# Hybrid backbone, one core: the instruction order planned by the scheduler's timeline model

## The chip, the cores and the metric

The kernel runs on one core of one Trainium2 chip. Such a core has a matrix engine (TensorE, PE in the profile), three engines for element-wise work (VectorE = DVE, ScalarE = ACT, GpSimd = POOL), a queue engine that here only issues transfers (SyncE = SP), and 16 DMA engines. Each engine works through its own instruction list strictly in the order in which the program gives it; engines wait for each other by semaphores. The metric is the device time of the launch in microseconds (us); the kernel before takes 1644.6 us, the median of 3 runs (1644.48 to 1645.88).

## What is computed

Two layers of a transformer-like trunk, over 256 context tokens and 1024 latent tokens of width 1024, in float32. Layer 0 mixes tokens by windowed attention with grouped heads, layer 1 by multi-head latent attention (MLA). Cut to what matters here:

```python
def reference(x, c, ctx, c_ctx, ...):
    for i in range(DEPTH):                       # DEPTH = 2
        shift_x, scale_x, gate_x = adaln(c, ada_w[i], ada_b[i])
        hx = rms_norm(x, norm_g[i]) * (1.0 + scale_x[:, None]) + shift_x[:, None]
        hc = rms_norm(ctx, norm_g[i]) * (1.0 + scale_c) + shift_c
        if kind == 0:
            yx, yc = window_gqa(hx, hc, ...)     # layer 0
        elif kind == 1:
            yx, yc = latent_attention(hx, hc, ...)   # layer 1
        x = x + gate_x[:, None] * yx
    return rms_norm(x, final_g)

def latent_attention(...):                       # 16 heads, keys = ctx and latent tokens
    def attend(qn, qr, kn, kr, v):
        s = (jnp.einsum("bqhd,bkhd->bhqk", qn, kn)
             + jnp.einsum("bqhd,bkd->bhqk", qr, kr)).astype(F32) * scale
        p = jax.nn.softmax(s, axis=-1).astype(v.dtype)
        return jnp.einsum("bhqk,bkhd->bqhd", p, v)
```

## The kernel before

The kernel is written for Tile, a layer that records the instructions of a Python function, finds from the memory that each reads and writes what it depends on, and plans when the block closes: it lets a modelled clock run and gives each engine, whenever the model has it free, the ready instruction that stands first in the source. The result is a fixed list per engine, with semaphore waits between them. The model of time is thus what decides where the lists depart from the order of the source.

On-chip memory is cut by hand: one float32r area (`arena_r`), one float32 area (`arena_f`), small columns (`small`) and all eight banks of the accumulator memory as one tensor (`PB`). Products that need full precision are made of two float32r halves (`split`: a cast on ACT at L120, the rest by a subtraction on DVE or POOL at L121) and three matmuls (`mm3`, L125, L126, L127). The stages in order, with the stretch of the profiled span that each takes:

- 0 to 66 us, the start: the conditioning product (`ada_mm`, L301) waits for `ada_w` pieces from memory; tokens are loaded (L175), normalised, turned (L187).
- 66 to 366 us: layer 0's projections (`proj_a`, `proj_t`), weights loaded at L227; beside them DVE sums up the rest of the conditioning (L362, with its loads at L341).
- 366 to 729 us: windowed attention, 40 units (tile of 128 queries, group of 4 heads). Per unit: scores (L569, L570), their maximum on DVE (L576), exponential on ACT (L579), turning of the probabilities on PE (`T`, L597), cast and rest (L120, L121), the product with V (`PV`, L607). The output product of the tile before (`outproj`, three matmuls at a time through L125 to L127) is dealt out between them as filler, in eight portions of six matmuls per tile.
- 729 to 1013 us: layer 1's projections.
- 1013 to 1561 us: MLA, 32 units (head, half of the queries). Per unit ten chunks of 128 keys: scores of 128 keys by 512 queries (L1188, through `mm3`), exponential on ACT (L1190), sum on POOL (L1194, L1197). Ahead of that, for the unit after next or the next one, the `top` products (L1171) and their maximum (L1175 on DVE), turned at L1179. At the end the product with V (L1205), whose two accumulators sit in the upper and lower 64 rows of one bank.
- 1561 to 1646 us: the last output product and the final norm.

In MLA the product with V is 10 plain float32 matmuls, one per chunk, with 64 columns of weights each; even chunks use the columns 0 to 63 of the array, odd ones the columns 64 to 127. In the source they stand together, behind the tenth score:

```python
        def PV(self):
            self.pv = psv()
            for c in range(NT):
                p = 64 * (c % 2)
                nc.tensor.matmul(
                    self.pv[p : p + 64], Vq[:, c, self.h % 4, :], self.E.pop(c), start=c < 2, stop=c >= NT - 2
                )
...
            u.score(c)
...
            if c == 9:
                u.PV()
                u.fin()
```

`Er` holds ten exponentials, the scores turn through three banks (`pst4`), the product with V has one bank (`psv`, bank 6), and `fin` (L1219 on ACT, L1220 on DVE) empties it.

## Time and profile before

| what | value |
|---|---|
| median of 3 runs | 1644.6 us (1644.48 to 1645.88) |
| profiled execution, its own time | 1647.77 us |
| its span, first to last instruction | 1645.9 us |
| granted TensorE clock, mean | 0.990 |
| DVE / ACT / POOL busy | 964.1 / 825.2 / 792.5 us |
| bytes moved | 176.75 MB, mean 107 GB/s |

The profiled execution is 3.2 us longer than the median, and its span is 1.9 us shorter than its own time. PE has most of the span; the other three are busy for about half of it. A matmul in the records is longer than the distance to the next one, since they are pipelined, so the price of a matmul is read from one start to the next. A plain float32 matmul (L1205, L301) leaves two records in the trace, every other one leaves one.

### The profile page before, as it was taken

What the parts mean: (1) busy time and instruction counts of PE and PEld (TensorE: products, weight loads), DVE (VectorE), ACT (ScalarE), POOL (GpSimd) and SP (SyncE); (2) the same over time, 40 slices, a digit from 0 to 9 for tenths busy, and PEclk for the clock granted to TensorE, in tenths of its full rate; (3) what the DMA queues carried; (4) which work ended last, traced back from release to release, by engine and by line L of the source; (5) the groups of instructions that cost most, each with busy time, mean ns of one, the idle gap of its engine ahead of it and who ended that gap; (6) DMA issues with size and microseconds to landing.
All of it is one profiled execution on the core that took longest, in us unless ns stands there. A gap on an engine that the chain in (4) does not pass through costs nothing.

```text
span 1645.9 us, 23722 instructions
## 1 busy us (share of the span) xinstructions
PE 1587.9 (96%) x8156; PEld 1215.5 (74%) x8156; DVE 964.1 (59%) x1972; ACT 825.2 (50%) x1779; POOL 792.5 (48%) x776
## 2 busy tenths in 40 slices
PE   6899999999999999998999999999999999999998
PEld 2687778887878888878887887566756756666687
DVE  1797853539888888869454015655555455455354
ACT  3622112249777777777333334555555555555421
POOL 1444426224453333345254423686676777668510
PEclk9899999999999999999999999999999999999999
DMA  8557665364343333334127713111111111122151
GB/s 280 165 154 204 180 206 141 94 178 124 93 119 94 91 90 90 90 113 160 52 90 251 222 61 103 61 55 33 39 40 34 45 40 35 49 77 69 47 160 65
DMA packets 127202, 176.75 MB, mean 107 GB/s; under 512 B 11100, under 2 KB 69084, under 8 KB 127080
## 3 DMA queue, kind: packets, MB, share of 16 engines
q1 hardware_dynamic: 124920, 171.12, 34.4%
q10 hardware_dynamic: 2160, 4.11, 0.8%
q8 instruction: 64, 1.05, 0.3%
q14 instruction: 58, 0.48, 0.1%
HBM read 129.04 MB, written 46.15 MB: 106 GB/s over the span
## 4 chain that ended last, share of the span: by engine, by line
PE 70%; DVE 11%; ACT 6%; issue 6%; POOL 3%; DMA 3%; SPq 0%; ACTq 0%; DVEq 0%; POOLq 0%
PE PB L125 15%; PE PB L127 15%; PE PB L126 15%; PE PB L1205 9%; PE PB L1171 4%; PE PB L607 3%; PE PB L597 3%; DVE arena_f L362 2%; DVE arena_r L121 2%; PE PB L569 2%; DVE arena_f L576 1%; PE PB L570 1%; ACT arena_f L579 1%; DMA arena_f<-ada_w 1%; ACT arena_r L120 1%
## 5 line engine op out<-in xcount | busy, mean ns | idle before, releaser
L125 PE MATMUL PB<-arena_r 128*128 128x512 f32 (+3 forms) x1632 | 608.1, 373 | 5.7 <-ACT arena_r L204 3.8
L126 PE MATMUL PB<-arena_r 128*128 128x512 f32 (+3 forms) x1632 | 599.2, 368 | 4.0 <-DVE arena_r L206 3.6
L127 PE MATMUL PB<-arena_r 128*128 128x512 f32 (+3 forms) x1632 | 597.0, 368 | 0.2 <-DVE arena_r L121 0.2
L125 PEld LDWEIGHTS PB<-arena_r 128*128 128x128 f32 (+1 forms) x1632 | 311.2, 191 | 95.3 <-issue 30.3
L1197 POOL TENSOR_TENSOR arena_f<-arena_f 128x512 f32<-128x512 f32 x252 | 326.9, 1297 | 76.4 <-ACT arena_f L1190 61.3
L127 PEld LDWEIGHTS PB<-arena_r 128*128 128x128 f32 (+1 forms) x1632 | 310.9, 191 | 50.3 <-issue 0.9
L126 PEld LDWEIGHTS PB<-arena_r 128*128 128x128 f32 (+1 forms) x1632 | 312.2, 191 | 45.9 <-DVE arena_r L206 4.7
L1190 ACT ACTIVATE arena_f<-PB 128x512 f32<-128x512 f32 x320 | 188.9, 597 | 126.6 <-PE PB L127 114.7
L1175 DVE TENSOR_REDUCE arena_f<-PB 128x1 f32<-128x1280 f32 x128 | 190.5, 1488 | 105.4 <-PE PB L1171 102.9
L121 DVE TENSOR_TENSOR arena_r<-PB,arena_r 128x512 fp32r<-128x512 f32 (+4 forms) x255 | 162.3, 644 | 114.8 <-ACT arena_r L120 113.1
L121 POOL TENSOR_TENSOR arena_r<-arena_f,arena_r 128x512 fp32r<-128x512 f32 x84 | 117.6, 1412 | 153.5 <-ACT arena_r L120 106.5
L120 ACT CAST arena_r<-PB 128x512 fp32r<-128x512 f32 (+4 forms) x255 | 137.7, 549 | 66.6 <-PE PB L597 27.8
L576 DVE CUSTOM_DVE_ANT_0 arena_f<-PB,arena_f,small 128x256 f32<-128x256 f32 (+1 forms) x288 | 145.8, 523 | 28.1 <-PE PB L570 21.9
L1205 PE MATMUL PB<-arena_f 128*64 128x512 f32 x640 | 157.1, 600 | 0.0
L579 ACT ACTIVATE arena_f<-arena_f,small 128x640 f32<-128x640 f32 (+2 forms) x160 | 119.3, 747 | 28.8 <-DVE small L578 27.9
L120 ACT CAST arena_r<-arena_f 128x512 fp32r<-128x512 f32 (+2 forms) x132 | 78.3, 609 | 105.5 <-DMA arena_f<-a_w_in 21.3
L607 PE MATMUL PB<-arena_r 128*128 128x512 f32 x336 | 123.3, 441 | 4.3 <-ACT arena_f L618 3.2
L597 PE MATMUL PB<-ident,arena_f 128*128 128x128 f32 x672 | 110.6, 274 | 1.0 <-ACT arena_f L579 0.8
L1205 PEld LDWEIGHTS PB<-arena_f 128*64 128x64 f32 x640 | 43.5, 136 | 80.9 <-issue 79.7
L1171 PE MATMUL PB<-arena_r 96*128 96x512 f32 (+1 forms) x384 | 99.8, 368 | 2.0 <-DVE arena_f L1175 1.9
L362 DVE SCALAR_TENSOR_TENSOR arena_f<-arena_f,small 128x512 f32<-128x512 f32 x98 | 87.7, 942 | 17.7 <-DMA arena_f<-ada_w 17.5
L597 PEld LDWEIGHTS PB<-ident,arena_f 128*128 128x128 f32 x672 | 83.3, 140 | 19.3 <-ACT arena_f L579 4.7
(149 smaller groups left out, 1768.7 us busy)
## 6 DMA issues: line engine op xcount, KB each, us to landing
arena_r<-q_d SPq DMA_DIRECT2D x80, 256.0 KB
arena_f<-ada_w SPq DMA_DIRECT2D x68, 256.0 KB
arena_f<-a_w_in SPq DMA_DIRECT2D x40, 256.0 KB
q_d<-arena_f SPq DMA_DIRECT2D x80, 128.0 KB
arena_f<-x SPq DMA_DIRECT2D x16, 512.0 KB
qn_d<-arena_f SPq DMA_DIRECT2D x16, 512.0 KB
arena_r<-qn_d SPq DMA_DIRECT2D x32, 256.0 KB
arena_f<-ada_w SPq DMA_DIRECT2D x14, 512.0 KB
```

What stands on the lines that cost most here:

```text
L120: nc.scalar.copy(hi, src)
L121: (lo_eng or nc.vector).tensor_sub(lo, src, hi.bitcast(F32))
L125: nc.tensor.matmul(o, ah, bh, start=first, stop=False)
L126: nc.tensor.matmul(o, al, bh, start=False, stop=False)
L127: nc.tensor.matmul(o, ah, bl, start=False, stop=last)
L597: nc.tensor.transpose(pt[:, h, :], self.Ps[h][:, ci * 128 : ci * 128 + 128], ident)
L607: nc.tensor.matmul(self.pv, V[:, self.chunks[ci], self.g, :], PT[:, s], start=ci == 0 and s == 0, stop=ci == self.m - 1 and s == 1,)
L1171: nc.tensor.matmul(psm[:, n0 : n0 + n], self.qT[0:96, 0, b * 128 : b * 128 + 128], kt[0:96, 0, n0 : n0 + n], start=True, stop=True,)
L1175: nc.vector.reduce_max(self.mx[:, 96 + b : 97 + b], psm[:, 0:TOK], AX.X, negate=True)
L1190: nc.scalar.activation(E, S, AF.Exp)
L1197: eng.tensor_add(self.acc, self.acc, E)
L1205: nc.tensor.matmul(self.pv[p : p + 64], Vq[:, c, self.h % 4, :], self.E.pop(c), start=c < 2, stop=c >= NT - 2)
```

## The change

One argument of the context is set. Nothing in the kernel's function changes: the same 12744 instructions that do work or transfers, on the same engines, with the same operands.

```diff
-    with tile.TileContext(nc) as tc:
+    with tile.TileContext(nc, schedule_with_timeline_sim=True) as tc:
         tile_hybrid_backbone_kernel(tc, t, out)
```

With it the planner's clock is that of a model with a timeline for all engines, in place of the simpler one. Where an engine's next instruction by the source isn't ready by that clock, a later one is drawn ahead. Of PE's 7790 matmuls 5282 change their place, by 14 places on average over all; in the windowed attention by 30. Of 772 instructions on POOL 217 move, of 658 transfers on SP 313, most by a place or two.

PE in MLA, one unit (L125 to L127 are the three matmuls of one score, L1171 a `top`, L1205 the product with V). Before:

```order
L127 MATMUL PB<-arena_r 128x512
L1171 MATMUL PB<-arena_r 128x512 x2
L1171 MATMUL PB<-arena_r 128x256
L1205 MATMUL PB<-arena_f 64x512 x10
L125 MATMUL PB<-arena_r 128x512
L126 MATMUL PB<-arena_r 128x512
L127 MATMUL PB<-arena_r 128x512
L1171 MATMUL PB<-arena_r 128x512 x2
L1171 MATMUL PB<-arena_r 128x256
```

The ten products with V stand in one piece. Changed, the same engine and stage:

```order
L127 MATMUL PB<-arena_r 128x512
L1205 MATMUL PB<-arena_f 64x512
L125 MATMUL PB<-arena_r 128x512
L126 MATMUL PB<-arena_r 128x512
L127 MATMUL PB<-arena_r 128x512
L1205 MATMUL PB<-arena_f 64x512
L125 MATMUL PB<-arena_r 128x512
L126 MATMUL PB<-arena_r 128x512
L127 MATMUL PB<-arena_r 128x512
L1205 MATMUL PB<-arena_f 64x512
L1171 MATMUL PB<-arena_r 128x512 x2
L1171 MATMUL PB<-arena_r 128x256
```

Products with V are drawn between the scores as soon as their exponential is there, mostly one at a time. Over all 320 of them: before, 55 pieces (23 of ten, 2 of nine, 7 of six, 7 of two, 16 of one); now 218 pieces (3 of four, 22 of three, 49 of two, 144 of one), with even and odd chunks still taking turns.

PE in the middle of the windowed attention (L125 to L127 are the output product of the tile before, L569 and L570 a score, L597 turns, L607 the product with V, L626 turns the reciprocals). Before:

```order
L607 MATMUL PB<-arena_r 128x512 x2
L125 MATMUL PB<-arena_r 128x512
L126 MATMUL PB<-arena_r 128x512
L127 MATMUL PB<-arena_r 128x512
L125 MATMUL PB<-arena_r 128x512
L126 MATMUL PB<-arena_r 128x512
L127 MATMUL PB<-arena_r 128x512
L569 MATMUL PB<-arena_r 128x256
L570 MATMUL PB<-arena_r 128x256
L569 MATMUL PB<-arena_r 128x384
L570 MATMUL PB<-arena_r 128x384
L597 MATMUL PB<-ident,arena_f 128x128 x4
```

Now:

```order
L607 MATMUL PB<-arena_r 128x512
L125 MATMUL PB<-arena_r 128x512
L569 MATMUL PB<-arena_r 128x256
L570 MATMUL PB<-arena_r 128x256
L626 MATMUL PB<-ident,arena_f 128x128 x2
L126 MATMUL PB<-arena_r 128x512
L127 MATMUL PB<-arena_r 128x512
L125 MATMUL PB<-arena_r 128x512
L126 MATMUL PB<-arena_r 128x512
L127 MATMUL PB<-arena_r 128x512
L607 MATMUL PB<-arena_r 128x512
L597 MATMUL PB<-ident,arena_f 128x128 x2
```

The filler no longer comes in sixes at set places: it stands 73 places earlier on average, its longest piece is 19 matmuls instead of 6, and the two halves of a product with V can be parted.

SP at the start (L294 loads `ada_w`, L175 a tile of tokens, L227 layer 0's weights):

```order
 L227 DMA arena_f<-a_w_in 128x2x256 x2
+L294 DMA arena_f<-ada_w 128x2x512 x3
 L175 DMA arena_f<-x 128x1024
-L294 DMA arena_f<-ada_w 128x2x512 x4
+L294 DMA arena_f<-ada_w 128x2x512
 L175 DMA arena_f<-x 128x1024
-L294 DMA arena_f<-ada_w 128x2x512 x2
-L227 DMA arena_f<-a_w_in 128x2x256 x2
-L294 DMA arena_f<-ada_w 128x2x512 x2
+L294 DMA arena_f<-ada_w 128x2x512
+L227 DMA arena_f<-a_w_in 128x2x256 x2
```

Three of the `ada_w` pieces are issued ahead of a tile of tokens.

## The prediction

> **What bounds the kernel now.** First the page: engines, then the chain that ended last.
>
> ```profile
> span 1645.9 us, 23722 instructions
> PE 1587.9 (96%) x8156; PEld 1215.5 (74%) x8156; DVE 964.1 (59%) x1972; ACT 825.2 (50%) x1779; POOL 792.5 (48%) x776
> PE 70%; DVE 11%; ACT 6%; issue 6%; POOL 3%; DMA 3%; SPq 0%; ACTq 0%; DVEq 0%; POOLq 0%
> ```
>
> PE is busy for 96% of the span and holds most of the chain. A new order adds or removes no work, so it can act in two ways only: on PE's idle time, and on what the same matmuls cost beside other neighbours. The table of windows gives the first by stage (stretch, its length, then busy time of PE, PEld, DVE, ACT, POOL, granted clock, DMA share, GB/s):
>
> ```profile
> 0.00:66.00 66.00, 47.69 (x215) 24.86 (x216) 24.09 (x47) 27.23 (x52) 17.08 (x26) 0.90 0.71 241
> 66.00:366.00 300.00, 289.28 (x1537) 241.95 (x1536) 187.09 (x292) 80.80 (x147) 117.97 (x89) 0.98 0.58 164
> 366.00:729.00 363.00, 353.25 (x2080) 298.00 (x2080) 307.08 (x1060) 289.48 (x720) 153.51 (x214) 1.00 0.34 96
> 729.00:1013.00 284.00, 276.00 (x1422) 233.82 (x1421) 120.35 (x231) 114.56 (x235) 109.03 (x127) 0.99 0.43 139
> 1013.00:1561.00 548.00, 543.83 (x2542) 351.66 (x2541) 283.06 (x282) 293.22 (x583) 386.81 (x300) 1.00 0.16 51
> 1561.00:1646.00 85.00, 77.82 (x370) 65.24 (x368) 42.47 (x65) 19.90 (x44) 8.13 (x22) 0.99 0.34 111
> ```
>
> PE idles 18.3 us at the start, 10.7 in layer 0's projections, 9.8 in the windowed attention, 8.0 in layer 1's projections, 4.2 in MLA and 7.2 at the end. That is all that a better order can win: 46.8 us ahead of MLA, and next to nothing in MLA, where PE has work for 543.8 of 548 us. MLA is the longest stage, and there any matmul that gets dearer goes straight onto the end, since ACT with 293 and POOL with 387 busy microseconds have room.
>
> **What a product with V costs, alone and in company.** The changed order breaks the 320 products with V (L1205) from 55 pieces into 218. The timeline of PE shows pieces of one, two, six and ten in the kernel before (start, length, line; two records per matmul on L1205), the chain of waits a piece of nine:
>
> ```profile
> 1058.61 0.39 PE L127 MATMUL PB<-arena_r 100*128 100x512 f32 x1
> 1058.93 1.07 PE L1205 MATMUL PB<-arena_f 128*64 128x512 f32 x2
> 1059.93 0.31 PE L1179 MATMUL PB<-ident,arena_f 128*100 128x128 f32 x1
> ...
> 1062.20 2.80 PE L1205 MATMUL PB<-arena_f 128*64 128x512 f32 x12
> 1064.92 0.50 PE L125 MATMUL PB<-arena_r 100*128 100x512 f32 x1
> 1065.26 0.39 PE L126 MATMUL PB<-arena_r 100*128 100x512 f32 x1
> 1065.49 0.40 PE L127 MATMUL PB<-arena_r 100*128 100x512 f32 x1
> 1065.82 1.07 PE L1205 MATMUL PB<-arena_f 128*64 128x512 f32 x2
> 1066.82 0.50 PE L125 MATMUL PB<-arena_r 100*128 100x512 f32 x1
> 1067.15 0.39 PE L126 MATMUL PB<-arena_r 100*128 100x512 f32 x1
> 1067.38 0.40 PE L127 MATMUL PB<-arena_r 100*128 100x512 f32 x1
> 1067.71 1.08 PE L1205 MATMUL PB<-arena_f 128*64 128x512 f32 x4
> 1068.72 0.72 PE L1171 MATMUL PB<-arena_r 96*128 96x512 f32 x2
> ...
> 1078.82 4.51 PE L1205 MATMUL PB<-arena_f 128*64 128x512 f32 x20
> 1083.26 0.50 PE L125 MATMUL PB<-arena_r 100*128 100x512 f32 x1
> ```
> ```profile
> 1043.83 4.43 PE PB L1205 x18
> ```
>
> Read from the start of a piece to the start of what follows: one product takes 1.00 us (1058.93 to 1059.93, and again 1065.82 to 1066.82), two take 1.01, six 2.72, ten 4.44, and nine 4.43. One costs what two cost, and nine what ten cost. So an even and an odd chunk that stand next to each other run at the same time, in the two halves of the array, for 0.86 us the pair ((4.44 - 2.72) / 2 pairs); a product without a neighbour of the other half holds the array for the same 0.86. Each piece ends with another 0.15 (2.72 - 3 x 0.86 = 0.14, 4.44 - 5 x 0.86 = 0.14, 1.00 - 0.86 = 0.14). At its front the matmul ahead gets longer too: L127 to L1205 takes 0.32 and 0.33 us (1058.61 to 1058.93, 1065.49 to 1065.82, 1067.38 to 1067.71), L126 to L127 0.23, so 0.10 more. A piece of n products thus costs 0.25 us + 0.86 us x (n/2, rounded up).
>
> The Trainium skill has a rule that speaks against such an order: by "TensorEngine Tiling (Array Packing)", section "Key Properties", different tiles of the array compute in parallel, but a change of the tiling mode drains TensorE. The 0.25 us per piece agree with a drain; without one, the sum below would be 63.6 us instead of 104.4.
>
> **The sum for MLA.** Before: 23 pieces of ten, 2 of nine, 7 of six, 7 of two, 16 of one are 115 + 10 + 21 + 7 + 16 = 169 array times and 55 pieces: 169 x 0.86 + 55 x 0.25 = 159.1 us. As a check: a piece's own length in the timeline is 0.07 longer than the distance to the next start (1.07 for 1.00, 4.51 for 4.44), so without the 0.10 ahead of it L1205 should be busy 169 x 0.86 + 55 x 0.22 = 157.4 us. Its row in the table of windows has 157.1; the two rows under it are used below:
>
> ```profile
> 1013.00:1561.00 548.00, 157.06 (x640) 43.55 (x640) 1.00 0.16 51
> L1175 DVE TENSOR_REDUCE arena_f<-PB 128x1 f32<-128x1280 f32 x128 | 190.5, 1488 | 105.4 <-PE PB L1171 102.9
> L1190 ACT ACTIVATE arena_f<-PB 128x512 f32<-128x512 f32 x320 | 188.9, 597 | 126.6 <-PE PB L127 114.7
> ```
>
> Now: 144 of one, 49 of two, 22 of three, 3 of four are 144 + 49 + 44 + 6 = 243 array times and 218 pieces: 243 x 0.86 + 218 x 0.25 = 263.5 us. The difference is 74 x 0.86 + 163 x 0.25 = 63.6 + 40.8 = **+104.4 us** of PE time. Pieces of three do not occur in the trace; if their third product cost only half a pair, 22 x 0.43 = 9.5 us go off, so the term lies between 95 and 104. I take 103, since nine cost what ten do, and no cover exists: ACT waits 126.6 us for PE at L1190 and DVE 105.4 at L1175 (rows above), so neither is what PE would have waited for. Of PE's 4.2 idle microseconds here some 3 should go, since a score now stands further behind the exponential that empties its bank: **-3**.
>
> **The rest of the program.** The filler of the windowed attention is bunched. What PE waits for there are short chains, a cast and a subtraction behind each turn:
>
> ```profile
> L121 DVE TENSOR_TENSOR arena_r<-PB,arena_r 128x512 fp32r<-128x512 f32 (+4 forms) x255 | 162.3, 644 | 114.8 <-ACT arena_r L120 113.1
> L120 ACT CAST arena_r<-PB 128x512 fp32r<-128x512 f32 (+4 forms) x255 | 137.7, 549 | 66.6 <-PE PB L597 27.8
> L301 PE MATMUL PB<-arena_f,small 128*2 128x512 f32 x64 | 23.1, 663 | 7.8 <-DMA arena_f<-ada_w 7.8
> ```
>
> In the new order a few products with V stand right behind the turn that they need (the piece shown in the part on the change has L607 after a single one of two L597 groups); each such place costs up to the 0.55 us of a cast. On the other side the order draws scores ahead of the turns. DVE is the second engine of that stage, 307 of 363 us, so a stretch without filler shows as waiting. From below, all of the 9.8 idle microseconds go; from above, one cast per unit, 40 x 0.55 = 22 us. Nearer to the lower end in kind, since most places keep a whole chain between: I take **+3**. At the start PE waits 7.8 us for `ada_w`; three pieces of it now go ahead of a tile of tokens, which is then late instead: the bytes that the first 66 us need stay the same, and they move at 241 GB/s there. From -8 (that wait gone) to +8 (moved to the turns): **0**. The projections' stages keep their order nearly everywhere (counted in the two orders, 299 of the 1518 matmuls of layer 0's move): 0, from -9 to +9, half of their 18.7 idle microseconds.
>
> **Sum.** 103 - 3 + 3 = +103 us. On the profiled execution's own 1647.8 us that makes 1750.6; it is 3.2 us above the median, so **1747 us** beside 1644.6, 6% slower.
>
> **The rivals.**
>
> *The idle time is won back.* The timeline model follows all engines, and its order may fit the chip better ahead of MLA, with less waiting. There are 46.8 us to win; the start's 18.3 hang on transfers and hardly move, so half of the total is much: -23. 1747 - 23 - 3 (the windowed attention's) = 1721 us. Against it: the idle time there is spread over short waits that the kernel's own interleaving of the source already aimed at.
>
> *The windowed attention starves.* The filler is gone where the chains are long; at a cast per unit, 22 us instead of 3, and as much as half of 18.7 in the projections: 1747 + 19 + 9 = 1775 us.
>
> *The array pairs them anyway: not slower.* If an odd product could still overlap its even partner across the three matmuls of a score between them, the 63.6 us of lost pairing and most of the 40.8 would vanish, and with 23 us of idle time won the time would be 1644.6 - 23 + (0 to 20) = 1622 to 1642 us. It decides from about 80% of the term on. The rows at 1065.82 and 1067.71 speak against it: there an odd product stands three matmuls ahead of the next ones, just as in the new order, and each piece pays in full. By the Trainium skill, "TensorE: Matmul & The Clock Gate", section "The mechanism", weight loads may be pulled ahead but matmuls start and end in strict order; those rows agree.
>
> That the change does nothing is excluded by the order itself.
>
> **How the numbers follow.** Forecast (1735 to 1760): 0.76. Idle time won back: 0.10. Starved attention: 0.11. Paired anyway: 0.03. The range of 8 in 10 takes in the term's lower bound (95 instead of 103) together with most of the won idle time, and most of the starved case: 1720 to 1770 us. Anything beyond 0.2% (3.3 us), about what a measurement of this kernel can tell from no change, counts: faster 0.02, same 0.01, slower 0.97.
>
> **What would show it.** In the profile after: L1205's busy time in MLA near 257 us instead of 157 (243 x 0.86 + 218 x 0.22); single L1205 rows with 1.00 us to the next start; MLA some 100 us longer with PE busy almost throughout; the stages ahead of it within 10 us of their lengths. Wrong would be: pieces of one that take 0.43, an MLA stage of 548 us, or more than 20 us moved ahead of it.

## The result, and the profile after

| | median us | ratio to before, 95% interval |
|---|---|---|
| before | 1644.54 (4 runs) | |
| timeline model | 1797.17 (1796.0 to 1797.94, 4 runs) | 1.0928 [1.0909, 1.0947] |

The change costs 152.6 us. The forecast was slower, but by 103 us, and its range ended at 1770. The page of the profiled execution (1796.5 us) begins so:

```profile
span 1794.7 us, 23680 instructions
PE 1709.8 (95%) x8156; PEld 1214.4 (68%) x8156; DVE 950.7 (53%) x1972; ACT 830.9 (46%) x1779; POOL 790.1 (44%) x776
```

The other engines work as long as before (DVE 951 for 964 us, ACT 831 for 825, POOL 790 for 793). PE's busy time grows by 122 us with the same 8156 records, and its idle time from 58 to 85. The row of the products with V on the same page, and their busy time in MLA from the table of windows (stretch, length, PE, PEld, clock, DMA share, GB/s):

```profile
L1205 PE MATMUL PB<-arena_f 128*64 128x512 f32 x640 | 255.5, 615 | 0.0
```
```profile
1016.70:1703.90 687.20, 254.89 (x638) 49.30 (x640) 1.00 0.12 37
```

255.5 us instead of 157.1: the forecast was 257. The granted clock in MLA is 1.00 here as in the kernel before, so it is not the clock that makes them dearer. What one piece costs stands in the timeline of PE (start, length, line, count; two records per product):

```profile
1242.98 0.40 PE L127 MATMUL PB<-arena_r 100*128 100x512 f32 x1
1243.30 1.07 PE L1205 MATMUL PB<-arena_f 128*64 128x512 f32 x2
1244.31 0.50 PE L125 MATMUL PB<-arena_r 100*128 100x512 f32 x1
1244.64 0.39 PE L126 MATMUL PB<-arena_r 100*128 100x512 f32 x1
1244.87 0.40 PE L127 MATMUL PB<-arena_r 100*128 100x512 f32 x1
1245.20 1.07 PE L1205 MATMUL PB<-arena_f 128*64 128x512 f32 x2
...
1259.41 1.93 PE L1205 MATMUL PB<-arena_f 128*64 128x512 f32 x6
1261.27 0.50 PE L125 MATMUL PB<-arena_r 100*128 100x512 f32 x1
```

One product again takes 1.00 us to the next start (1243.30 to 1244.31 in rounded rows; all 144 pieces of one lie between 1.002 and 1.004), three take 1.86 (1259.41 to 1261.27). The matmul ahead takes 0.32 instead of 0.23 (1242.98 to 1243.30), as forecast. So does, and this the forecast left out, the one behind: L125 to L126 is 0.33 (1244.31 to 1244.64), L126 to L127 0.23. A piece between scores thus costs 0.35 us beside its array times, not 0.25.

The second surprise stands at the end of a unit. This is the timeline of PE, ACT and DVE around the turn L1179, first in the kernel before (rows of other lines left out):

```profile
1214.26 0.27 PE L1179 MATMUL PB<-ident,arena_f 128*100 128x128 f32 x1
1214.29 0.47 PE L127 MATMUL PB<-arena_r 100*128 100x512 f32 x1
1214.60 0.76 PE L1171 MATMUL PB<-arena_r 96*128 96x512 f32 x3
1214.69 1.12 ACT L1182 ACTIVATE arena_r<-PB,ident 4x128 fp32r<-4x128 f32 x4
1215.29 4.51 PE L1205 MATMUL PB<-arena_f 128*64 128x512 f32 x20
...
1219.73 0.50 PE L125 MATMUL PB<-arena_r 100*128 100x512 f32 x1
```

and then in the changed one:

```profile
1186.78 0.27 PE L1179 MATMUL PB<-ident,arena_f 128*100 128x128 f32 x1
1186.81 0.84 PE L1171 MATMUL PB<-arena_r 96*128 96x512 f32 x3
1187.58 1.12 ACT L1182 ACTIVATE arena_r<-PB,ident 4x128 fp32r<-4x128 f32 x4
1187.68 1.49 DVE L1175 TENSOR_REDUCE arena_f<-PB 128x1 f32<-128x1280 f32 x1 [1.03 <-PE PB L1171]
1188.75 0.50 PE L125 MATMUL PB<-arena_r 100*128 100x512 f32 x1 [1.11 <-ACT arena_r L1182]
```

L1179 turns the maxima of the next unit's scores; ACT writes them in four steps into that unit's queries (L1182), and only then can its first score start. Before, the ten products with V stood between turn and score, 4.4 us of work. Now they have been drawn ahead, one `top` of 0.6 us is left, and PE stands for 1.11 us. The waits of PE (waiter, awaited line, total us, times, longest) show it 20 times:

```profile
PE PB L125 <- ACT arena_r L1182: 21.1, 20, 1.9
```

In the kernel before, PE has no wait at L1182 among its groups. The table of windows shows the same, and more (stretch, length, PE, PEld, DVE, ACT, POOL, clock, DMA share, GB/s):

```profile
722.00:950.00 228.00, 212.42 (x1082) 180.78 (x1082) 99.99 (x207) 98.01 (x201) 96.54 (x115) 0.97 0.45 147
950.00:1036.00 86.00, 79.52 (x363) 59.65 (x361) 29.57 (x34) 31.42 (x57) 24.27 (x21) 0.94 0.28 87
1036.00:1679.00 643.00, 619.82 (x2377) 321.19 (x2376) 259.07 (x256) 273.64 (x541) 363.27 (x285) 1.00 0.12 35
```

In MLA (the last row) PE idles 23.2 us, where the kernel before had 4.2. In the stages ahead of it PE idles 15.6 and 6.5 us, and the granted clock is 0.97 and 0.94; in the kernel before the stretches 719 to 949 and 949 to 1020 us have 8.7 us at 0.99 and 0.2 us at 1.00.

By stage, with each matmul's time up to the next matmul's start given to the stage that its source line belongs to (us; the trace's rows laid beside the program's order, the same rule for all kernels below; the head of MLA is what the source puts between layer 1's projections and the loop over the 32 units):

| stage | before | after | difference |
|---|---|---|---|
| start | 61.5 | 57.4 | -4.1 |
| layer 0's projections | 299.8 | 291.6 | -8.2 |
| windowed attention | 363.2 | 363.6 | +0.4 |
| layer 1's projections | 223.5 | 232.8 | +9.3 |
| head of MLA | 61.6 | 69.4 | +7.8 |
| MLA | 535.7 | 675.5 | +139.8 |
| end | 88.6 | 92.9 | +4.3 |

MLA has 140 of 149 us. By the prices read off: 74 array times x 0.86 = 63.6; 163 pieces x 0.25 = 40.8 (as forecast), x 0.10 behind them = 16.3; the wait at L1182 21.1. That is 141.8, 2 us more than measured.

### The profile page after: what moved, and what is told of

It is laid out like the page before. It is cut to its first block, busy times and chain, and to the rows that moved or that the text cites. A ratio compares the mean times of both kernels' runs of the same rounds, so it can differ in the third digit from the quotient of the medians.

```text
span 1794.7 us, 23680 instructions
## 1 busy us (share of the span) xinstructions
PE 1709.8 (95%) x8156; PEld 1214.4 (68%) x8156; DVE 950.7 (53%) x1972; ACT 830.9 (46%) x1779; POOL 790.1 (44%) x776
## 4 chain that ended last, share of the span: by engine, by line
PE 52%; ACT 2%; DVE 2%; DMA 1%; issue 1%; POOL 0%; SPq 0%; POOLq 0%; ACTq 0%; DVEq 0%
PE PB L1205 13%; PE PB L125 12%; PE PB L126 11%; PE PB L127 11%; PE PB L1171 4%; ACT arena_r L1182 1%; PE PB L1230 1%; DVE arena_f L201 1%; PE PB L1248 0%; DVE arena_r L206 0%; DMA arena_f<-b_w_out 0%; ACT arena_r L120 0%; DMA arena_f<-b_w_in 0%; DVE arena_f L1175 0%; ACT arena_f L1219 0%
## 5 line engine op out<-in xcount | busy, mean ns | idle before, releaser
L125 PE MATMUL PB<-arena_r 128*128 128x512 f32 (+3 forms) x1632 | 618.6, 381 | 31.2 <-ACT arena_r L1182 21.1
L126 PE MATMUL PB<-arena_r 128*128 128x512 f32 (+3 forms) x1632 | 598.7, 367 | 5.9 <-DVE arena_r L206 5.7
L127 PE MATMUL PB<-arena_r 128*128 128x512 f32 (+3 forms) x1632 | 595.8, 366 | 0.0
L125 PEld LDWEIGHTS PB<-arena_r 128*128 128x128 f32 (+1 forms) x1632 | 309.8, 191 | 197.9 <-ACT arena_f L1190 66.5
L1197 POOL TENSOR_TENSOR arena_f<-arena_f 128x512 f32<-128x512 f32 x252 | 323.6, 1284 | 160.6 <-ACT arena_f L1190 151.6
L127 PEld LDWEIGHTS PB<-arena_r 128*128 128x128 f32 (+1 forms) x1632 | 310.8, 191 | 48.1
L126 PEld LDWEIGHTS PB<-arena_r 128*128 128x128 f32 (+1 forms) x1632 | 312.0, 191 | 44.5 <-DVE arena_r L206 8.1
L1190 ACT ACTIVATE arena_f<-PB 128x512 f32<-128x512 f32 x320 | 191.1, 598 | 269.5 <-PE PB L127 263.8
L1175 DVE TENSOR_REDUCE arena_f<-PB 128x1 f32<-128x1280 f32 x128 | 190.4, 1488 | 235.8 <-PE PB L1171 234.3
L121 DVE TENSOR_TENSOR arena_r<-PB,arena_r 128x512 fp32r<-128x512 f32 (+5 forms) x255 | 162.3, 643 | 185.6 <-ACT arena_r L120 184.0
L1205 PE MATMUL PB<-arena_f 128*64 128x512 f32 x640 | 255.5, 615 | 0.0
L120 ACT CAST arena_r<-PB 128x512 fp32r<-128x512 f32 (+5 forms) x255 | 136.0, 552 | 90.7 <-PE PB L127 35.9
L121 POOL TENSOR_TENSOR arena_r<-arena_f,arena_r 128x512 fp32r<-128x512 f32 x84 | 115.0, 1384 | 141.2 <-ACT arena_r L120 82.5
L607 PE MATMUL PB<-arena_r 128*128 128x512 f32 x336 | 125.1, 432 | 4.1 <-ACT arena_r L120 1.8
L597 PE MATMUL PB<-ident,arena_f 128*128 128x128 f32 x672 | 108.5, 275 | 3.2 <-ACT arena_f L579 2.6
L1205 PEld LDWEIGHTS PB<-arena_f 128*64 128x64 f32 x640 | 49.3, 135 | 91.1 <-issue 90.5
L1171 PE MATMUL PB<-arena_r 96*128 96x512 f32 (+1 forms) x384 | 106.7, 385 | 1.6 <-DVE arena_f L1175 1.6
L1194 POOL TENSOR_TENSOR arena_f<-arena_f 128x512 f32<-128x512 f32 x32 | 41.1, 1283 | 143.5 <-ACT arena_f L1190 143.5
L1171 PEld LDWEIGHTS PB<-arena_r 96*128 96x128 f32 x384 | 64.5, 191 | 56.0 <-issue 39.8
```

The costliest lines, as they stand in the source:

```text
L120: nc.scalar.copy(hi, src)
L121: (lo_eng or nc.vector).tensor_sub(lo, src, hi.bitcast(F32))
L125: nc.tensor.matmul(o, ah, bh, start=first, stop=False)
L126: nc.tensor.matmul(o, al, bh, start=False, stop=False)
L127: nc.tensor.matmul(o, ah, bl, start=False, stop=last)
L607: nc.tensor.matmul(self.pv, V[:, self.chunks[ci], self.g, :], PT[:, s], start=ci == 0 and s == 0, stop=ci == self.m - 1 and s == 1,)
```

## The experiments

The theory to test: MLA loses by the price of the pieces (0.86 us per array time, 0.35 per piece) and by the lost cover of the turn, and both are PE's order alone. The rival: the timeline model's order on DVE, ACT and SP carries a good part. It has room for that: beside the moves on PE, POOL and SP named above, 1150 of ACT's 1573 instructions and most of DVE's change their place too. Stage times of all kernels, as above (kernels 1 to 4, 7 and 8 were run once each, 5, 6 and 9 four times, 10 ten times; beside them the kernel before took 1644.1 us in one run for 1 to 4, 1639.6 to 1649.4 for 5 and 6, 1645.1 to 1650.4 for 7 to 10):

| kernel | start | proj. 0 | window | proj. 1 | head | MLA | end | time |
|---|---|---|---|---|---|---|---|---|
| before | 61.5 | 299.8 | 363.2 | 223.5 | 61.6 | 535.7 | 88.6 | 1644.5 |
| after | 57.4 | 291.6 | 363.6 | 232.8 | 69.4 | 675.5 | 92.9 | 1797.2 |
| 1 whole pieces | 57.0 | 291.5 | 364.4 | 234.6 | 71.5 | 550.5 | 95.3 | 1678.1 |
| 2 pair behind the turn | 58.5 | 291.9 | 363.1 | 231.2 | 70.2 | 688.2 | 90.6 | 1807.5 |
| 3 singles in the source | 59.7 | 302.2 | 363.1 | 223.4 | 61.7 | 654.9 | 90.3 | 1768.9 |
| 4 pairs in the source | 61.7 | 300.2 | 363.1 | 223.4 | 61.7 | 552.7 | 89.1 | 1665.5 |
| 5 layer 1 in source order | 57.1 | 292.2 | 372.2 | 231.9 | 75.4 | 590.1 | 88.6 | 1725.5 |
| 6 all of PE in source order | 63.2 | 288.7 | 391.2 | 233.8 | 74.8 | 597.8 | 88.6 | 1752.9 |
| 7 PE as before | 63.5 | 293.7 | 371.2 | 223.2 | 62.1 | 547.4 | 88.6 | 1663.1 |
| 8 PE as after, old model | 60.1 | 296.7 | 399.1 | 242.6 | 66.4 | 673.2 | 93.3 | 1845.8 |
| 9 start as after | 56.0 | 293.0 | 363.0 | 224.0 | 61.6 | 533.2 | 88.6 | 1634.4 |
| 10 the same, glued | 57.4 | 291.4 | 362.9 | 223.3 | 61.7 | 552.4 | 88.6 | 1653.1 |

### 1. The pieces made whole again

```diff
-                nc.tensor.matmul(
+                mm = nc.tensor.matmul(
                     self.pv[p : p + 64], Vq[:, c, self.h % 4, :], self.E.pop(c), start=c < 2, stop=c >= NT - 2
                 )
+                if True:
+                    tc.keep_in_program_order(mm)
```

> The changed kernel, with each product with V of MLA (L1205) tied behind the matmul traced before it, so that the ten stand nearly whole: 53 pieces and 161 array times instead of 218 and 243. Theory (the loss is the price of the pieces, 0.86 us per array time and 0.35 per piece, and the 21 us that PE waits for ACT's L1182 because the products with V no longer stand behind the turn L1179): 82 x 0.86 + 165 x 0.35 = 128 us less and no wait at L1182, so 1797 - 149 = about 1648 us. Rival (a third of the loss is the timeline model's order elsewhere, on DVE, ACT and SP): only the 104 us of my forecast come back, about 1693 us.

Measured: 1678.1 us, between the two. MLA falls from 675.5 to 550.5, by 125 us; the theory had 128 for the pieces and 21 for the wait. The wait at L1182 fell only to 12.8 us, since in a part of the units the turn now stands behind the glued piece:

```profile
PE PB L125 <- ACT arena_r L1182: 12.8, 14, 1.3
```

And the other stages keep the changed kernel's times: layer 1's projections, head and end are 28 us above before. Some 117 of the 125 us are thus not this wait, near the price of the pieces; what happens in the other stages is still open here.

### 2. The cover given back alone

```diff
-            nc.tensor.transpose(pm[0:100], self.mx[:, 0:100], ident)
+            UnitB.turned = nc.tensor.transpose(pm[0:100], self.mx[:, 0:100], ident)
...
+                if c == 8:
+                    tc.add_manual_dep(mm.ins, UnitB.turned.ins.name, NOSYNC, reason="behind the shift")
+                if c == 9:
+                    tc.keep_in_program_order(mm)
```

`NOSYNC` stands here for a dependency that fixes the order without a semaphore.

> The changed kernel, with the last pair of the products with V tied behind the next unit's turn L1179; the others go as the model likes and are now even more broken: 251 pieces and 256 array times instead of 218 and 243. Theory (two separate prices): 13 x 0.86 + 33 x 0.35 = 22.7 us more for the pieces, and the 21.1 us at L125 behind L1182 gone, so about 1799 us, with PE's wait for L1182 under 3 us. Rival (the wait at L1182 only shows where PE stops in any case, and moves on to another place): 1797 + 23 = about 1820 us.

Measured: 1807.5 us, between 1799 and 1820. The wait for L1182 went from 21.1 to under a microsecond, as the theory says, and L1205's busy time rose to 274.7 us, the price of more pieces:

```profile
L125 PE MATMUL PB<-arena_r 128*128 128x512 f32 (+3 forms) x1632 | 618.8, 381 | 9.9 <-ACT arena_r L204 6.3 <-ACT arena_f L1190 1.0 <-ACT arena_r L1182 0.8
L1205 PE MATMUL PB<-arena_f 128*64 128x512 f32 x640 | 274.7, 620 | 0.0
```
```profile
PE PB L1179 <- DVE arena_f L1175: 16.4, 19, 1.7
```

But a wait one link earlier grew to 16.4 us (4.1 in the changed kernel): PE now stands at the turn, for DVE's maximum. The rival was half right. What lacks cover is the whole chain `top`, maximum (1.49 us), turn, four steps on ACT (1.12 us and the way there), first score. The pair that was put back covered one link only.

### 3 and 4. Singles and pairs, written in the source of the kernel before

The planner is the old one; `PV` is cut into single products, called from the loop over chunks. For the singles:

```diff
+    PVAT = {4: (0,), 5: (1,), 6: (2,), 7: (3,), 8: (4,), 9: (5,), 10: (6, 7, 8, 9)}
...
             u.score(c)
+            for k in PVAT.get(c, ()):
+                u.PV1(k)
             if nnu and c == 9:
                 nnu.top(0)
             if c == 9:
-                u.PV()
+                for k in PVAT[10]:
+                    u.PV1(k)
                 u.fin()
```

and for the pairs `PVAT = {5: (0, 1), 7: (2, 3), 9: (4, 5), 10: (6, 7, 8, 9)}`.

> The kernel before with its own planner, and the first six products with V written singly between the scores of the source, the last four together behind the tenth score: 221 pieces and 256 array times instead of 55 and 169. Theory (it is the pieces, whoever plans them; four products behind the turn cover L1182): 87 x 0.86 + 166 x 0.35 = 133 us more, about 1777 us. Rival (the timeline model's other moves carry a good part of the 152 us): clearly less than 133 us more, about 1745 us or under, as the forecast's price of 0.25 per piece and a partly shared array would give.

> The kernel before with its own planner, and the first six products with V written in pairs (one even, one odd chunk) between the scores, the last four together: 126 pieces and 161 array times instead of 55 and 169. Theory (an array time is shared by an even and an odd product next to each other): -8 x 0.86 + 71 x 0.35 = 18 us more, about 1662 us. Rival (every break costs about the same, 152 us over 163 more pieces = 0.93 us, whether or not it parts a pair): 71 x 0.93 = 66 us more, about 1711 us.

Measured: 1768.9 and 1665.5 us, that is 124 and 21 us above before, where the prices sum to 133 and 18. The old model with products broken about as much thus loses 124 of the 152.6 us, and the first rival is out by 24 us. Between the two kernels the number of pieces falls from 221 to 126 and the array times from 256 to 161: 103 us for 95 pieces and 95 array times, 1.09 us for one of each where the prices say 1.21. A break that parts a pair is thus far dearer than one that leaves the pairs whole, by about the array time; the second rival, 66 us for the pairs, is out too.

The singles tell something of the cover as well. Four products stand behind the turn there, and PE has no wait at L1182 and none at the turn: from 1016 to 1681 us it is busy for 664.8 of 665 us. The singles stay 9 us under their sum, and 14 under it in MLA alone (654.9 for 535.7). About 4 of these are the idle time that the kernel before had in MLA (4.2 us) and this one has not; the rest is open.

L1205's busy time with singles and with pairs (its line is L1210 there):

```profile
L1210 PE MATMUL PB<-arena_f 128*64 128x512 f32 x640 | 267.2, 612 | 0.0
```
```profile
L1210 PE MATMUL PB<-arena_f 128*64 128x512 f32 x640 | 166.2, 613 | 0.0
```

### 5 and 6. PE in the order of the source

All matmuls and turns go through a helper that ties each to the one traced before it on PE, from the start of layer 1 or from the first instruction:

```diff
+    pin = [False]
+    def pe_matmul(*a, **k):
+        i = nc.tensor.matmul(*a, **k)
+        return tc.keep_in_program_order(i) if pin[0] else i
...
+    pin[0] = True
     pst = Banks(6, 7)
```

> The changed kernel, with every matmul and turn on PE tied to the order of the source from the start of layer 1 on (32 whole pieces of ten, 160 array times); layer 0 and the other engines stay as the timeline model plans them. Theory (PE's order is the whole cause in layer 1; DVE, ACT and SP follow): layer 1's projections back from 232.8 to about 223 us, the head of MLA from 69.4 to 62, MLA from 675.5 to about 530 (160 array times and 32 pieces are 16 us less than before, of which some returns as waits), the end from 92.9 to 89; the start and layer 0's projections keep their gain of 12 us: about 1630 to 1640 us, faster than before. Rival (the order on DVE, ACT and SP carries the rest of the loss): layer 1's projections, the head and the end stay some 20 us long, about 1655 us.

> The changed kernel with every matmul and turn on PE tied to the order of the source in the whole program. Theory (the start and layer 0's projections gained 12 us by PE's order, that is by doing what is ready while ada_w is on its way): that gain goes, the rest as in the kernel that is tied from layer 1 on, so 10 to 15 us more than that one, about 1645 to 1650 us. Rival (the gain came from the order of the transfers on SP and of DVE): it stays, and the two tied kernels are within 4 us of each other.

Measured: 1725.5 us (ratio 1.0474 [1.0445, 1.0504]) and 1752.9 us (1.0653 [1.0618, 1.0689]). Both theories missed, by 90 and by 100 us. I had taken the order of the source for that of the kernel before; it isn't. The old planner moves 1968 of PE's 7790 matmuls against the source, and with these tied back PE stands where it had gone on, and the granted clock of the profiled execution falls from 0.986 to 0.971 and 0.968. In the first of the two (the helper's lines are L85 for matmuls and L89 for turns, `split` is L131):

```profile
PE PB L85 <- DVE arena_r L131: 26.6, 15, 2.1
PE PB L89 <- DVE arena_r L131: 16.8, 9, 3.6
PE PB L89 <- ACT arena_f L1250: 12.9, 11, 1.2
```

MLA has the dearest matmuls in 32 whole pieces here and still takes 590 us. These two say nothing of the other engines' order; they led to the next pair. The second hypothesis, on what gained at the start, is left undecided by them too: the start lost 6 us when tied, the projections did not.

### 7 and 8. PE's order of one kernel, all else planned by the other's model

A table with the order of PE's 7790 matmuls, taken from one program, ties each to the one ahead of it; no other engine is tied.

```diff
         tile_hybrid_backbone_kernel(tc, t, out)
+        tie(tc, nc)
...
+def tie(tc, nc):
+    by = {i.name: i for i in nc.cur_bb.bb.instructions}
...
+        for a, b in zip(names, names[1:]):
+            tc.add_manual_dep(by[b], by[a].name, dep(), reason="order")
```

> The changed kernel with PE's whole order tied to that of the kernel before, matmul by matmul; the timeline model plans DVE, ACT, POOL and SP around it. Theory (all of the loss is PE's order, which broke the pieces and took the cover from the turn L1179): within 10 us of before, 1640 to 1655 us. Rival (the order on the other engines carries the 30 us by which the kernel with whole pieces stayed above before): about 1675 us.

> The kernel before, planned by its own model, with PE's whole order tied to that of the changed kernel; DVE, ACT, POOL and SP are planned by the old model around it. Theory (PE's order is the whole loss): 1785 to 1800 us, with PE's wait for L1182 near 21 us and L1205 busy 255 us. Rival (30 us belong to the other engines): about 1765 us.

Measured: 1663.1 and 1845.8 us. With PE as before, 134 of the 152.6 us are gone, and layer 1's projections (223.2), the head (62.1) and the end (88.6) are back within 0.5 us: what these lost went with PE's order as well, though experiment 1 had left it open. With PE as after, MLA takes 673.2 us under the old model, 675.5 under the new one, and PE waits at L1182 for 19.8 us:

```profile
PE PB L125 <- ACT arena_r L1182: 19.8, 20, 1.1
PE PB L569 <- DVE small L576: 12.7, 19, 2.0
```

So MLA's loss is settled: it follows PE's order, whoever plans the rest. Both kernels are slower than their own theory in another stage. Where PE's list comes from one clock and DVE's and ACT's from another, the windowed attention takes 371 and 399 us instead of 363, and in the first kernel MLA 12 us more, mostly PE behind DVE's L121 (8.1 us):

```profile
PE PB L125 <- DVE arena_r L121: 8.1, 7, 1.2
PE PB L569 <- DVE small L576: 7.7, 9, 1.9
```

The lists of the engines have to fit each other, it seems; that part isn't put on one engine here. PE in one kernel's order with all four others exactly in the other's was not tried.

### 9 and 10. A version that takes the better part of each

The same table, for all five engines: the changed order up to the end of layer 0's projections, the order before from there on. In the second kernel the products with V of a unit are also glued, at the place of their last piece.

> All five engines tied: up to the end of layer 0's projections to the order of the changed kernel, from there on to that of the kernel before (the first 1644 of 7790 matmuls, 299 DVE, 175 ACT, 104 POOL instructions and 255 transfers). Theory (the changed order is better by 12 us there, 61.5 + 299.8 against 57.4 + 291.6, and nothing later depends on it): 1644 - 12 = about 1632 us, ratio about 0.993. Rival (those 12 us are scatter of the transfers, which differ from run to run at the start): within 4 us of before.

> As the kernel whose start and projections follow the changed order, and in MLA the products with V of each unit glued into one piece of ten where its last piece stood in the kernel before (32 pieces and 160 array times instead of 55 and 169). Theory (0.86 per array time, 0.35 per piece): 9 x 0.86 + 23 x 0.35 = 15.8 us less than its sibling if nothing else waits, so about 1616 us. Rival (the single products had been drawn ahead because PE had nothing else, so what they filled comes back as a wait): no more than 4 us less.

Measured against 1646.75 us for before on the same chip: 1634.4 us, ratio 0.9929 [0.9911, 0.9947], and 1653.1 us, ratio 1.0036 [1.0025, 1.0047]. The first is faster than both kernels, by 0.7%: the 12 us that were read off. The start takes 56.0 us instead of 61.5, the projections 293.0 instead of 299.8, the rest about what it took.

In the second kernel the price of the pieces should have given 15.8 us, but MLA takes 19 us more than its sibling: the single products had covered K's split, and PE now waits for it. The wait is not all: where PE had stood for 2.04 us (in brackets below), a piece of ten then takes 6.41 us instead of 4.51, and the granted clock in that stretch is 0.50 (third value from the end of the row of windows):

```profile
PE PB L125 <- DVE arena_r L121: 14.3, 7, 2.0
```
```profile
1047.44 0.80 PE L125 MATMUL PB<-arena_r 100*128 100x512 f32 x1 [2.04 <-DVE arena_r L121]
1050.30 6.41 PE L1205 MATMUL PB<-arena_f 128*64 128x512 f32 x20
```
```profile
1049.00:1052.50 3.50, 3.50 (x10) 1.32 (x10) 0.00 (x0) 0.74 (x2) 2.53 (x2) 0.50 0.40 112
```
```profile
L1205 PE MATMUL PB<-arena_f 128*64 128x512 f32 x640 | 151.6, 622 | 0.0
```

Behind five of the seven waits the clock is 0.50 for 3.4 to 6.8 us, 20 us in all, and the mean in MLA is 0.98 for the sibling's 1.00. L1205 goes to 151.6 us only, where 160 whole array times and 32 pieces would be 144.6. So 14.3 us of waits at L121, 4.3 more at the turn and some 10 us of slow clock (half of 20, an estimate) stand against the 15.8 saved; some 6 of the 19 us stay open.

The 16 single products of the kernel before were thus not waste.

## Why the prediction fell short, step by step

*What bounds the kernel* was right: 140 of 149 us came in MLA, on PE, with ACT, POOL and DVE about as busy as before.

*Array times and pieces* were right. A piece of three takes what four take (1.86 and 1.87 us), L1205's busy time came out at 255.5 us for 257, and the rival in which the array pairs products across a score is out: every single one took 1.00 us.

*The price of a piece was mis-sized: "a piece of n products thus costs 0.25 us + 0.86 us x (n/2, rounded up)".* It is 0.35. The row that shows it stood in the prediction itself: 1066.82 to 1067.15 is 0.33 us for L125 behind a piece, with 0.23 next to it. I took the distance to the next start for the end of the cost and did not look one matmul further. 163 x 0.10 = 16.3 us.

*The step that failed: "no cover exists ... so neither is what PE would have waited for", and -3.* ACT and DVE did have room; but I asked only whether they were busy, and not what the products with V themselves covered. They were the work between the turn L1179 and the next unit's first score. Drawn ahead, they left PE 21.1 us of waits at L1182; instead of losing 3 of its 4.2 idle microseconds, PE idles 23.2 in MLA. Experiment 2 shows that the wait goes when a pair comes back, and that the link before it then shows 16.4 us; with four products behind the turn, as in experiment 3, both are gone. The two rows that the forecast rested on were also read a little high: of ACT's 126.6 us at L1190 114.7 ended with PE, of DVE's 105.4 at L1175 102.9. The forecast asked what the filler of the windowed attention hides, and did not ask it of the products with V.

*The rest of the program, forecast +3, came to +9.5:* the start and layer 0's projections won 12.3 us (forecast 0), the windowed attention lost 0.4 (forecast +3), layer 1's projections, the head of MLA and the end lost 21.4 (forecast 0). That the sum is no further off is luck: two misses of opposite sign. The last two were not looked at in the order at all, and of the projections only layer 0's were counted, with 299 of 1518 matmuls moved; by the same count 588 of the 1116 matmuls of layer 1's projections move. Experiment 7 shows that it is with PE's order that the three lost; in the profile the loss shows as idle time of PE and a lower clock (the rows from 722 to 1036 us above). The first rival, idle time won back, was half right for the start and layer 0's projections: PE's idle time up to their end falls by 6.9 us (29.0 to 22.2), and its busy time by another 6.1 (336.9 to 330.8), at a granted clock of 0.98 for 0.97. Experiment 9 keeps just that part. The windowed attention's +3 rested on a reading that the order shown does not bear out: no turn of probabilities (L597) stands ahead of the product with V (L607) in it.

Forecast 103; measured 152.6: +16 behind the pieces, +24 at L1182 (21 instead of -3), +6.5 elsewhere make 149.5. That is about the difference of the two profiled executions (148.8 us in span); the other 3 us are that the one before was 3.2 us above its median. The forecast's own last sum is off by 0.2 us (1647.8 + 103 is 1750.8), which changes nothing.

## What to carry to other kernels

A planner that sees readiness but not what neighbours cost each other can break up matmuls that run in parallel halves of the array, as here; before an order is changed, count the pieces and read the price of a piece up to the second instruction behind it, not only to its end. For every block of work that is drawn ahead, ask what it stood in front of: its place may have been the cover of a chain on idle engines. An idle PE can cost more than the wait, where the clock granted behind it is lower. Plans of two models can be joined at a stage's end where the sets of instructions up to the joint are the same; here that was worth 0.7%.

## What the runs showed of the hardware

- Plain float32 products of 64 weight columns, on alternating halves of the array: 0.86 us for a pair or for one alone; a parted pair pays it twice.
- Going from full-width float32r matmuls to such products and back costs 0.10 us ahead, 0.15 at the end and 0.10 in the matmul behind, whatever the length of the piece (one 1.00, two 1.01, three 1.86, four 1.87, ten 4.44 us to the next start). The 0.10 behind is that of a score or a `top` (0.33 instead of 0.23 us); a turn behind a piece takes 0.07 instead of 0.03. These products differ from the scores in their columns and in their type, and no run here tells which of the two makes the price.
- In experiment 10, behind five of seven waits of 2.04 us, the granted clock was 0.50 for 3.4 to 6.8 us, and the products within a piece took up to 0.85 instead of 0.43 us to the next start. In MLA of the changed kernel, with 20 waits of at most 1.9 us, the mean stayed at 1.00.
